# Dilated attention on one core: softmax weights transposed on TensorE and stored as 48 rows of 512 bytes, with buffers of their own for plain v, weight rows and probabilities

## The chip, the cores and the metric

The kernel runs on one core of one Trainium2 chip. The metric is the time of one execution on the device in microseconds (us), as a median over runs.

## The reference, cut to what matters

The program is two blocks of a transformer on 1024 rows of width 1024 in float32. The change lies in the first mixer of the first block, a dilated window attention with 18 heads in three groups of six. Each group has its own window and dilation. The three groups' outputs for one head are weighted by a softmax over the groups' log-sum-exps, multiplied with silu of a gate, and projected:

```
outs, lses = [], []
for g, (window, dil) in enumerate(DIL_GROUPS):          # 3 groups
    o, l = dilated_window_attention(q[:, :, hs], k[:, :, hs], v[:, :, hs], rel_bias[:, hs], window, dil)
    outs.append(o); lses.append(l)
wts = softmax(stack(lses, axis=0), axis=0)              # one weight for each group, row and head
o = concatenate([outs[g] * wts[g][..., None] for g in range(3)], axis=2)
y = o.reshape(B, S, WIDTH_A) * silu(gate)
return y @ w_out
```

The rest of the first block (a second mixer) and the whole second block follow after it and are not touched.

## The kernel before

Each float32 operand of a large product is split into a high and a low part, so that one product is three matmul passes. A weight tile comes by DMA into a raw buffer from one ring of five (`raw()`, shown as `wr`, 128 x 1024), a CAST makes its high part (`wh`, L199, on VectorE = DVE) and a subtraction its low part (`wl`, L203, on GpSimd = POOL or DVE).

The dilated stage walks nine pairs (hp, g): hp = 0, 1, 2 is a pair of heads in each group, g the group. For each pair, `dil_batches` gives a list of jobs (scores, softmax, transposes, values). Between the jobs the program issues "pieces" of other matmul work (`fill`): the q, k, v projection of the next pair, and, once a head pair is through all three groups, its three gates (`dil_gate`: 48 matmuls for each, in two halves of 24, each into one PSUM buffer `g`, of which there are two, then `th` by ScalarE = ACT and `sg` by DVE, L293) and three products (`dil_product`).

For each head pair hp, `dil_weights` reads the statistics of the three groups back from DRAM (`std`, L810), makes the softmax weights in a raw buffer with 16 small DVE operations and an Exp (L813 to L822), and stores them to DRAM (`wtd`, L825) so that each (group, head) is one row of 1024 numbers. In the raw buffer a partition is a row of the sequence within a tile, so that this store writes six times 1024 single numbers. `dil_product` then reads a row back into 64 partitions at a time (L528, two reads for each product), multiplies `sg` with it (L529) and with the attention's output (L530), and stores the result to DRAM (`yTa`, L532). Head pair 0 has its weights made in the first job of hp = 1, head pair 1 in that of hp = 2, and head pair 2 after the last job.

After that the output projection begins. `tail_begin` loads the nine rows of `a_w_out` in 512 KB pieces through the raw ring (L1097), multiplies each by a modulation row (L1098) and splits it. `tail_finish` has for each of eight tiles of 128 rows a `product(t, 0)` over the six early row blocks (head pairs 0 and 1: 36 matmuls of 512 columns) and a `product(t, 1)` over the three late ones (head pair 2: 18 matmuls). Each reads its part of `yTa` back (`yr`, L1157), and ACT casts it (`yh`, L1158).

Two queues set the order: nearly all DMAs are issued by SyncE (SP) in program order, and DVE, ACT, POOL and TensorE (PE) each work through their instructions in order. In order to load ahead, the weights of the following gate or projection are asked for when the one before starts (`next_w`). The lines that matter:

```
def raw(self, shape=None):
    return self.wr.tile(shape or [P, 1024], F32, tag="wr", bufs=5, name=self.nm("wr"))
...
for g in range(3):
    for a in range(2):
        nc.sync.dma_start(wtd[hp, g, a, :].rearrange("(t p) -> p t", p=P), z[:, :, a, g])
```

Of the kernel before, what the change touches and what calls it, by code (L numbers as in the profile page):

```python
# [12 lines left out]
F32 = mybir.dt.float32  # L13
F32R = mybir.dt.float32r
# [127 lines left out]
class Kern:  # L142
# [189 lines left out]
    def phase_A(self, x_in):  # L332
        nc, i = self.nc, self.i
        with ExitStack() as ctx:
# [93 lines left out]
            c1 = ExitStack()  # L428
            self.psum(c1, "", "so")
            ag = self.tags(ctx, "ag")  # L430
            lp = Pools(self.tags(c1, "al", side="right"), {t: ag for t in ("sg", "wb", "xs", "o")})
            yT = self.dr.tile([WA, S], F32, name="yTa")
            std = self.dr.tile([3, S, 12], F32, name="std")
            wtd = self.dr.tile([3, 3, 2, S], F32, name="wtd")
            parts = [([3 * g + hp for g in range(3)], yT.rearrange("(g h p) n -> h g p n", g=3, p=P)[hp])
                     for hp in range(3)]
            w_in = i["a_w_in"][0]
# [37 lines left out]
            for j, (hp, g) in enumerate(groups):  # L475
                jobs = self.dil_batches(lp, hp, g, tbd, std, qkv[j], os)
                pieces = 12
                if hp and g == 0:
                    for gg in range(3):
                        more += [gates[hp - 1, gg], self.dil_product(lp, hp - 1, gg, sgs, os, wtd, yT)]  # L480
                        pieces += 5
                more += [fills[j + 1]] if j < 8 else [gates[2, 0]]
                if j == 8:
                    pieces = 4
                done = 0
                for m, job in enumerate(jobs):
                    n = pieces * (m + 1) // len(jobs) - done
                    step(job, n)
                    if m == 0 and hp and g == 0:
                        self.dil_weights(lp, hp - 1, std, wtd)  # L490
                    done += n
                    next(mods, None)
                if j < 8:
                    fill(100)
            step(None, 0)
            self.dil_weights(lp, 2, std, wtd)
            self.next_w(3 * WA + 2 * 384 + 2 * P)
            self.pin = False
            c1.close()
            ct = ExitStack()  # L500
            tail = self.tail_begin(ct, parts[:2], i["a_w_out"][0], 0, nc.vector)
            for g in range(3):
                for _ in itertools.chain(gates[2, g], self.dil_product(lp, 2, g, sgs, os, wtd, yT)):
                    pass
        return self.tail_finish(ct, tail, parts[2:], i["a_w_out"][0], x_in, 0)

    def dil_gate(self, lp, ut, w_in, hp, g, sgs):
# [14 lines left out]
    def dil_product(self, lp, hp, g, sgs, os, wtd, yT):  # L522

        nc = self.nc
        sg = sgs[hp, g]
        wb = self.raw()
        for a in range(2):
            nc.sync.dma_start(wb[a * 64:(a + 1) * 64, :], wtd[hp, g, a, :].partition_broadcast(64))  # L528
        nc.vector.tensor_tensor(sg, sg, wb, OP.mult)  # L529
        (nc.vector if hp == 2 else nc.gpsimd).tensor_tensor(sg, sg, os[hp, g], OP.mult)  # L530
        c0 = g * 384 + hp * P
        nc.sync.dma_start(yT[c0:c0 + P, :], sg)  # L532
        yield
# [66 lines left out]
    def dil_project(self, lp, ut, w_in, hp, g, res):  # L600


        nc = self.nc
        dil = DILS[g]
        c0 = g * 384 + hp * P

        def perm(ap):
            return ap.rearrange("p (i d) -> p d i", d=dil)

        def flat(ap):  # L610
            return ap.rearrange("p (d i) -> p d i", d=dil)

        hl = S // dil // 2
        halves = [slice(0, hl), slice(hl, 2 * hl)]
        out = res[hp * 3 + g] = []

        def project(c, h, evac, tag):
            w = self.next_w(c)
            self.next_w(c, 1)
            ps = self.pp(tag, 2)  # L620
            for k0 in (0, 4):
                self.gemm_T_half(w, ut, h, ps, kts=range(k0, k0 + 4))
                if k0:
                    evac(h, perm(ps))
                yield

        def tiles(*names):
            return [lp.tile([P, S], F32R, tag=n, bufs=2, name=self.nm(n)) for n in names]

        def split_q(q):  # L630

            def evac(h, ps):
                for r, o, t in zip(rows, rows[::-1], q):
                    nc.scalar.copy(flat(t[r])[:, :, halves[h]], ps[r])
                for r, o, t in zip(rows, rows[::-1], q):
                    nc.vector.tensor_tensor(flat(t[o])[:, :, halves[h]], ps[r],
                                            flat(t[r])[:, :, halves[h]].bitcast(F32), OP.subtract)
            return evac

        def split_k(k, low):  # L640

            def evac(h, ps):
                for r, t in zip(rows, k):
                    nc.scalar.copy(flat(t[r])[:, :, halves[h]], ps[r])
                for r, o, t, u in zip(rows, rows[::-1], k, low):
                    for d in (r, o):
                        nc.vector.tensor_tensor(flat(u[d])[:, :, halves[h]], ps[r],
                                                flat(t[r])[:, :, halves[h]].bitcast(F32), OP.subtract)
                for r, o, t in zip(rows, rows[::-1], k):
                    nc.scalar.copy(flat(t[o])[:, :, halves[h]], ps[r])  # L650
            return evac

        rows = [slice(a * 64, a * 64 + 64) for a in range(2)]
        q, k, low = tiles("q0", "q1"), tiles("k0", "k1"), tiles("kl0", "kl1")
        out += [q, (k, low)]
        evacs = [split_q(q), split_k(k, low)]
        vt = self.raw()
        evacs.append(lambda h, ps: nc.scalar.copy(flat(vt)[:, :, halves[h]], ps))

        first = hp + g == 0  # L660
        order = [(j, h) for h in range(2) for j in range(3)]
        for j, h in order if first else sorted(order):
            yield from project(j * WA + c0, h, evacs[j], "t" if first and (j, h) == (2, 0) else "g")
        vh = lp.tile([P, NT, P], F32R, tag="vh", bufs=2, name=self.nm("vh"))
        vl = lp.tile([P, NT, P], F32R, tag="vl", bufs=2, name=self.nm("vl"))
        out.append((vh, vl))
        for h in range(2):
            tp = self.pp("t", 2, [P, 4, P])
            self.transposes(tp, vt[:, h * 512:(h + 1) * 512], 4)
            self.split(vh[:, h * 4:h * 4 + 4], vl[:, h * 4:h * 4 + 4], tp)  # L670
        yield

    def dil_batches(self, lp, hp, g, tbd, std, qkv, os):
# [72 lines left out]
        class Job:  # L746
# [27 lines left out]
            def transpose(self):  # L774
                rows, nb, nblk = self.rows, len(self.tl), self.nblk
                tp = kern.pp("t", 2, [P, 4, P])
                for j in range(nb):
                    for b in range(nblk):
                        kern.tr(tp[:, j * nblk + b, :rows], self.xs[:rows, j, b * P:(b + 1) * P],
                                kern.ident[:rows, :rows])  # L780
                self.ph = lp.tile([P, 4, P], F32R, tag="pth", bufs=1, name=kern.nm("pth"))
                self.pl = lp.tile([P, 4, P], F32R, tag="ptl", bufs=1, name=kern.nm("ptl"))
                m = nb * nblk
                kern.split(self.ph[:, :m, :rows], self.pl[:, :m, :rows], tp[:, :m, :rows])

# [19 lines left out]
    def dil_weights(self, lp, hp, std, wtd):  # L805

        nc = self.nc
        wb = self.raw()
        st = wb[:, 0:96].rearrange("p (t a g s) -> p t a g s", t=NT, a=2, g=3)
        nc.sync.dma_start(st, std[hp].rearrange("(t p) (a g s) -> p t a g s", p=P, a=2, g=3))  # L810
        mn, zz = (wb[:, c:c + 16].rearrange("p (t a) -> p t a", a=2) for c in (96, 112))
        e, z = (wb[:, c:c + 48].rearrange("p (t a g) -> p t a g", a=2, g=3) for c in (128, 176))
        nc.vector.tensor_reduce(mn, st[:, :, :, :, 0], AX.X, OP.min)  # L813
        for g in range(3):
            nc.vector.tensor_tensor(e[:, :, :, g], mn, st[:, :, :, g, 0], OP.subtract)
        nc.scalar.activation(e, e, AF.Exp)
        for g in range(3):
            nc.vector.tensor_tensor(z[:, :, :, g], e[:, :, :, g], st[:, :, :, g, 1], OP.mult)
        nc.vector.tensor_reduce(zz, z, AX.X, OP.add)
        nc.vector.reciprocal(zz, zz)  # L820
        for g in range(3):
            nc.vector.tensor_tensor(z[:, :, :, g], e[:, :, :, g], zz, OP.mult)  # L822
        for g in range(3):
            for a in range(2):
                nc.sync.dma_start(wtd[hp, g, a, :].rearrange("(t p) -> p t", p=P), z[:, :, a, g])  # L825


    def rope_pairs(self, eng, a, b, cos, sin, pool, shp):
# [1067 lines left out]

# [9 lines left out]
```

## Time and profile before

| what | value |
|---|---|
| median of 3 runs | 4132.61 us (4131.44 to 4135.64) |
| profiled execution, its own time | 4131.9 us |
| its span | 4130.1 us |
| granted TensorE clock, mean | 0.97 of full |
| PE busy | 3858.2 us, 93% of the span |
| DVE busy | 2447.7 us, 59% |
| ACT busy | 1382.1 us, 33% |
| POOL busy | 1085.5 us, 26% |

The profiled execution's own time is 1.8 us above its span and 0.7 us below the median. PE is the engine with the largest share. The dilated stage's part that is touched lies between about 225 and 745 us of the span; what comes after it is 82% of the span.

### The profile page before, as it was taken

To read this page: it belongs to the slowest core of one execution; us is meant where nothing else is said; L and a number is where in the kernel's file an instruction comes from. 1 tells how busy PE (TensorE), PEld (TensorE's weight loads), DVE (VectorE), ACT (ScalarE), POOL (GpSimd) and SP (SyncE) were. 2 spreads that over 40 slices of the span, in tenths; PEclk is the share of its full clock that TensorE was granted. 3 is DMA by queue.
4 is the path that set the end of the run, shared out by engine and by line. 5 is a ranking of instruction groups with operands and counts; after the bars stand their busy time and mean duration, and the time that the engine had idled before them with its cause. 6 is when DMAs were issued, how large, how long until landed. Compare 5 with 4: busy or idle time off the path is not lost. (4 is left out here: it accounts for less than half of the span.)

```text
span 4130.1 us, 54373 instructions
## 1 busy us (share of the span) xinstructions
PE 3858.2 (93%) x21085; PEld 3272.8 (79%) x21085; DVE 2447.7 (59%) x4596; ACT 1382.1 (33%) x2938; POOL 1085.5 (26%) x1016
## 2 busy tenths in 40 slices
PE   7979796899999989999999999997999999999998
PEld 5767675688889867999778888885999778888886
DVE  6645455956777767568754434338568764443436
ACT  3424242124777633256421111113136431111111
POOL 1111111420222322134233232334134232323233
PEclk9989898999999989999999999998999999999999
DMA  6363516220111243111421111113111231111112
GB/s 237 96 82 83 76 41 149 95 86 29 35 25 32 62 120 117 41 38 37 137 83 48 45 51 41 51 50 120 55 42 37 95 115 46 47 46 51 41 51 82
DMA packets 318897, 290.80 MB, mean 70 GB/s; under 512 B 70779, under 2 KB 273267, under 8 KB 318638
## 3 DMA queue, kind: packets, MB, share of 16 engines
q1 hardware_dynamic: 313362, 268.23, 23.5%
q10 hardware_dynamic: 5276, 19.08, 1.5%
q8 instruction: 167, 2.74, 0.3%
q14 instruction: 92, 0.75, 0.1%
HBM read 240.26 MB, written 51.72 MB: 71 GB/s over the span
## 5 line engine op out<-in xcount | busy, mean ns | idle before, releaser
L203 POOL TENSOR_TENSOR wl<-wr,wh 128x1024 fp32r<-128x1024 f32 (+1 forms) x253 | 495.4, 1966 | 1589.6 <-DVE wh L199 1502.8
L199 DVE CAST wh<-wr 128x1024 fp32r<-128x1024 f32 x222 | 181.9, 820 | 751.7 <-PE y L151 310.7
L151 PE MATMUL y<-uh_m,wl 128*128 128x512 f32 x1056 | 417.1, 395 | 4.7 <-DVE z L1631 4.2
L151 PE MATMUL y<-uh_m,wh 128*128 128x512 f32 x1056 | 419.8, 398 | 0.0
L151 PE MATMUL y<-ul_m,wh 128*128 128x512 f32 x1056 | 418.8, 397 | 0.0
L1784 ACT ACTIVATE cv<-y,cw 128x1024 f32<-128x1024 f32 x66 | 79.8, 1209 | 775.7 <-PE y L151 775.7
L151 PE MATMUL g<-uh_a,wl 128*128 128x512 f32 x568 | 236.8, 417 | 55.2 <-DVE sg L293 55.1
L151 PEld LDWEIGHTS y<-uh_m,wl 128*128 128x128 f32 x1056 | 199.0, 188 | 55.1 <-issue 4.6
L151 PEld LDWEIGHTS y<-uh_m,wh 128*128 128x128 f32 x1056 | 199.1, 189 | 48.4
L151 PEld LDWEIGHTS y<-ul_m,wh 128*128 128x128 f32 x1056 | 198.9, 188 | 47.6 <-DVE ul_m L191 0.9
L151 PE MATMUL y<-wo,yh 128*128 128x512 f32 x784 | 219.8, 403 | 17.0 <-ACT yh L1158 17.0
L151 PE MATMUL g<-ul_a,wh 128*128 128x512 f32 x568 | 229.3, 404 | 0.5 <-POOL ul_a L422 0.4
L151 PE MATMUL g<-uh_a,wh 128*128 128x512 f32 x568 | 228.7, 403 | 0.0
L151 PEld LDWEIGHTS y<-wo,yh 128*128 128x128 f32 x784 | 149.2, 193 | 50.7 <-ACT yh L1158 18.5
L191 DVE TENSOR_TENSOR pt<-t,pt 128x512 fp32r<-128x512 f32 x256 | 165.8, 680 | 22.2 <-ACT pt L190 20.4
L151 PE MATMUL y<-wl,hh 128*128 128x512 f32 x440 | 175.4, 399 | 0.0
L151 PE MATMUL y<-wh,hl 128*128 128x512 f32 x440 | 175.1, 398 | 0.0
L151 PE MATMUL y<-wh,hh 128*128 128x512 f32 x440 | 175.1, 398 | 0.0
L151 PEld LDWEIGHTS g<-uh_a,wl 128*128 128x128 f32 x568 | 111.5, 196 | 78.9 <-DVE sg L293 49.5
L995 DVE TENSOR_REDUCE nm<-s 128x1 f32<-128x1024 f32 x128 | 155.7, 1216 | 27.1 <-PE s L151 26.5
L151 PE MATMUL g<-wl,uh_f 128*128 128x256 f32 x576 | 166.4, 289 | 3.0 <-DVE dv L191 2.5
L151 PE MATMUL g<-wl,uh_n 128*128 128x256 f32 x576 | 166.0, 288 | 3.1 <-DVE dv L191 2.5
(446 smaller groups left out, 10312.2 us busy)
## 6 DMA issues: line engine op xcount, KB each, us to landing
wr<-w_up SPq DMA_DIRECT2D x88, 512.0 KB
wr<-ada_w SPq DMA_DIRECT2D x48, 512.0 KB
wr<-w_down SPq DMA_DIRECT2D x44, 512.0 KB
wr<-a_w_in SPq DMA_DIRECT2D x36, 512.0 KB
wr<-w_in SPq DMA_DIRECT2D x24, 512.0 KB
xs<-wr SPq DMA_DIRECT2D x16, 512.0 KB
wr<-xs ACTq DMA_DIRECT2D x16, 512.0 KB
wr<-w_in SPq DMA_DIRECT2D x32, 256.0 KB
```

The source lines that it names most:

```text
L151: ins = self.nc.tensor.matmul(*args, **kw)
L191: nc.vector.tensor_tensor(lo, src, hi.bitcast(F32), OP.subtract)
L199: (self.nc.scalar.copy if act else self.nc.vector.tensor_copy)(hi, raw)
L203: (eng or self.nc.gpsimd).tensor_tensor(lo[..., cs], raw[..., cs], hi[..., cs].bitcast(F32), OP.subtract)
L995: nc.vector.tensor_reduce(nm, sp, AX.X, OP.max, negate=True)
L1784: nc.scalar.activation(t, ps, AF.Identity, bias=cw[:, 3, c:c + 1], scale=cw[:, 2, c:c + 1])
```

## The change

- `dil_weights` works in an own tile `dw` (128 x 224) in place of a raw buffer, and writes the weights so that the 48 numbers of a partition are ordered (group, head, tile).
- The six stores are replaced by a generator `turn`: PE transposes the 128 x 48 weights into PSUM buffer `t`, DVE copies the 48 x 128 result into a tile `dz`, and one DMA stores 48 rows of 512 bytes. `turn` is one more piece of work that is issued behind the first gate of the head pair.
- The weight rows are read into an own single buffer `wb` and no longer into a raw buffer; a projection's plain v lies in an own single buffer `vt`.
- The probabilities' high and low parts (`pth`, `ptl`) have two buffers each in place of one.
- At the end of the stage the order of code was gate 0, product 0, gate 1, product 1, gate 2, product 2 of head pair 2. It is now gate 0, gate 1, `turn`, product 0, product 1, gate 2, product 2.
- A scratch size for dynamic DMAs is given.

Not changed: the 8-byte writes of the statistics to `std`, the read of `std`, the number of matmuls of the products.

```diff
-            lp = Pools(self.tags(c1, "al", side="right"), {t: ag for t in ("sg", "wb", "xs", "o")})
+            lp = Pools(self.tags(c1, "al", side="right"), {t: ag for t in ("sg", "wb", "xs", "o", "dw", "dz")})
...
-            wtd = self.dr.tile([3, 3, 2, S], F32, name="wtd")
+            wtd = self.dr.tile([3, 3, 2, NT, P], F32, name="wtd")
...
                 if hp and g == 0:
+                    turn_w = []
                     for gg in range(3):
                         more += [gates[hp - 1, gg], self.dil_product(lp, hp - 1, gg, sgs, os, wtd, yT)]
                         pieces += 5
+                    more.insert(1, itertools.chain.from_iterable(turn_w))
+                    pieces += 1
...
-                        self.dil_weights(lp, hp - 1, std, wtd)
+                        turn_w.append(self.dil_weights(lp, hp - 1, std, wtd))
...
-            self.dil_weights(lp, 2, std, wtd)
+            turn_w = self.dil_weights(lp, 2, std, wtd)
...
-            for g in range(3):
-                for _ in itertools.chain(gates[2, g], self.dil_product(lp, 2, g, sgs, os, wtd, yT)):
-                    pass
+            last = [self.dil_product(lp, 2, g, sgs, os, wtd, yT) for g in range(3)]
+            for _ in itertools.chain(gates[2, 0], gates[2, 1], turn_w, *last[:2], gates[2, 2], last[2]):
+                pass
...
-        wb = self.raw()
+        wb = lp.tile([P, S], F32, tag="wb", bufs=1, name=self.nm("wb"))
         for a in range(2):
-            nc.sync.dma_start(wb[a * 64:(a + 1) * 64, :], wtd[hp, g, a, :].partition_broadcast(64))
+            nc.sync.dma_start(wb[a * 64:(a + 1) * 64, :], wtd[hp, g, a].rearrange("t p -> (t p)").partition_broadcast(64))
...
-        vt = self.raw()
+        vt = lp.tile([P, S], F32, tag="vt", bufs=1, name=self.nm("vt"))
...
-                self.ph = lp.tile([P, 4, P], F32R, tag="pth", bufs=1, name=kern.nm("pth"))
-                self.pl = lp.tile([P, 4, P], F32R, tag="ptl", bufs=1, name=kern.nm("ptl"))
+                self.ph = lp.tile([P, 4, P], F32R, tag="pth", bufs=2, name=kern.nm("pth"))
+                self.pl = lp.tile([P, 4, P], F32R, tag="ptl", bufs=2, name=kern.nm("ptl"))
...
-        wb = self.raw()
+        wb = lp.tile([P, 224], F32, tag="dw", bufs=1, name=self.nm("dw"))
...
-        e, z = (wb[:, c:c + 48].rearrange("p (t a g) -> p t a g", a=2, g=3) for c in (128, 176))
+        e = wb[:, 128:176].rearrange("p (t a g) -> p t a g", a=2, g=3)
+        z = wb[:, 176:224].rearrange("p (g a t) -> p t a g", a=2, g=3)
...
-        for g in range(3):
-            for a in range(2):
-                nc.sync.dma_start(wtd[hp, g, a, :].rearrange("(t p) -> p t", p=P), z[:, :, a, g])
+
+        def turn():
+
+            ps = self.pp("t", 2)
+            self.tr(ps[:48, :P], wb[:, 176:224], self.ident)
+            rows = lp.tile([48, P], F32, tag="dz", bufs=1, name=self.nm("dz"))
+            nc.vector.tensor_copy(rows, ps[:48, :P])
+            nc.sync.dma_start(wtd[hp].rearrange("g a t p -> (g a t) p"), rows)
+            yield
+
+        return turn()
...
-    nc = bacc.Bacc("TRN2", target_bir_lowering=False, num_devices=1)
+    nc = bacc.Bacc("TRN2", target_bir_lowering=False, num_devices=1, dynamic_dma_scratch_size=1024)
```

The first place is SP's queue around the weights of head pair 0. The numbers in a name only tell one buffer from another; `wr_2313` before and `wr_2324` after are the same load, the weights of the gate (0, 2). Before, from the statistics' last writes on:

```order
L744 DMA std<-stats_1745 512x1x2
L217 DMA wr_2162<-a_w_in 128x8x128
L744 DMA std<-stats_1745 512x1x2
L810 DMA wr_2216<-std 128x8x12
L825 DMA wtd<-wr_2216 128x8x1 x6
L528 DMA wr_2281<-wtd 64x1024 x2
L217 DMA wr_2313<-a_w_in 128x8x128
L528 DMA wr_2407<-wtd 64x1024 x2
```

The same stretch of SP's queue in the changed kernel, whose read of the statistics is L813, store L834 and read of the weight rows L531:

```order
L217 DMA wr_2324<-a_w_in 128x8x128
L560 DMA wr_2436<-ada_b 1x1024
L696 DMA T_2142<-tbd 128x384
L747 DMA std<-stats_1748 512x1x2 x2
L545 DMA wr_2515<-ada_w 128x1024
L813 DMA dw_2222<-std 128x8x12
L545 DMA wr_2567<-ada_w 128x1024
L737 DMA std<-stats_2141 64x2
L738 DMA std<-stats_2141 64x2
L834 DMA wtd<-dz_2286 48x128
L217 DMA wr_2594<-a_w_in 128x8x128
L531 DMA wb_2318<-wtd 64x1024 x2
```

The gate's weight load stood behind the six stores and the first read of weight rows; it now stands ahead of the last writes of the statistics.

The second place is SP's queue at the end of the stage. Before, it runs from the first row of `a_w_out` on:

```order
L1097 DMA wr_5345<-a_w_out 128x1024
L825 DMA wtd<-wr_5299 128x8x1 x6
L1097 DMA wr_5355<-a_w_out 128x1024
L1097 DMA wr_5362<-a_w_out 128x1024
L1097 DMA wr_5369<-a_w_out 128x1024
L1097 DMA wr_5376<-a_w_out 128x1024
L1157 DMA yr_5568<-yTa 128x3x128
L1097 DMA wr_5383<-a_w_out 128x1024
L1157 DMA yr_5568<-yTa 128x3x128
L528 DMA wr_5390<-wtd 64x1024 x2
```

In the changed kernel the first four rows of `a_w_out` (L1109 there) have been issued further up; from the last writes of the statistics on, SP has:

```order
L747 DMA std<-stats_5065 512x1x2 x2
L1109 DMA wr_5388<-a_w_out 128x1024
L813 DMA dw_5309<-std 128x8x12
L1109 DMA wr_5549<-a_w_out 128x1024
L1109 DMA wr_5559<-a_w_out 128x1024
L1109 DMA wr_5566<-a_w_out 128x1024
L1169 DMA yr_5633<-yTa 128x3x128 x2
L834 DMA wtd<-dz_5454 48x128
L531 DMA wb_5457<-wtd 64x1024 x2
L1169 DMA yr_5828<-yTa 128x3x128 x2
L531 DMA wb_5463<-wtd 64x1024
L535 DMA yTa<-sg_5099 128x1024
```

All nine loads of `a_w_out` now stand ahead of the store of the weights, where eight stood behind the six stores.

The third place is DVE's queue at the end of the stage, in the changed kernel, from the seventh row of `a_w_out` (L1110 is the product with the modulation row) to the copy of the turned weights (L833); ahead of it, behind the last split of probabilities (`ptl`, L191), stand a subtraction L203, L817, two more L1110 and the three L819:

```order
L1110 TENSOR_TENSOR wr_5549<-wr_5549,wr_5348 128x1024
L822 TENSOR_TENSOR dw_5309<-dw_5309 128x8x2 x3
L199 CAST wo_5391<-wr_5388 128x1024
L823 TENSOR_REDUCE dw_5309<-dw_5309 128x16
L203 TENSOR_TENSOR wo_5392<-wr_5388,wo_5391 128x1024
L824 RECIPROCAL dw_5309<-dw_5309 128x16
L293 SCALAR_TENSOR_TENSOR sg_5397<-th_5422,g_5395 128x512
L826 TENSOR_TENSOR dw_5309<-dw_5309 128x8x2 x3
L1110 TENSOR_TENSOR wr_5559<-wr_5559,wr_5348 128x1024
L1110 TENSOR_TENSOR wr_5566<-wr_5566,wr_5348 128x1024
L1172 TENSOR_TENSOR yl_5589<-yr_5581,yh_5585 128x384 x2
L833 COPY dz_5454<-t_5452 48x128
```

Before, the small operations on the weights followed the last `ptl` at once, with no work on `a_w_out` between them; now the copy stands behind five L1110, one CAST and two L203.

## Rows read from the trace of the kernel before

**Rows 1.** Page: busy time of each engine over the whole span.

```profile
PE 3858.2 (93%) x21085; PEld 3272.8 (79%) x21085; DVE 2447.7 (59%) x4596; ACT 1382.1 (33%) x2938; POOL 1085.5 (26%) x1016
```

**Rows 2.** Timeline, PE (start us, us, instruction [idle before <-releaser]), waits over 4 us.

```profile
237.67 1.11 PE L156 MATMUL t<-ident,xs 128*128 128x128 f32 x4 [6.61 <-DVE vl L191]
...
275.28 0.79 PE L151 MATMUL g<-uh_a,wl 128*128 128x512 f32 x1 [14.82 <-DVE sg L293]
...
491.12 0.79 PE L151 MATMUL g<-uh_a,wl 128*128 128x512 f32 x1 [18.70 <-DVE sg L293]
...
655.45 0.77 PE L151 MATMUL g<-uh_a,wl 128*128 128x512 f32 x1 [6.82 <-DVE sg L293]
...
677.91 0.79 PE L151 MATMUL g<-uh_a,wl 128*128 128x512 f32 x1 [14.71 <-DVE sg L293]
...
705.79 2.07 PE L151 MATMUL y<-wo,yh 128*128 128x512 f32 x4 [11.23 <-ACT yh L1158]
...
725.70 2.08 PE L151 MATMUL y<-wo,yh 128*128 128x512 f32 x4 [4.54 <-ACT yh L1158]
```

**Rows 3.** Windows: us, busy time of each engine, granted clock, DMA share, GB/s.

```profile
core 0: us, PE busy (x) PEld busy (x) DVE busy (x) ACT busy (x) POOL busy (x), PEclk, DMA share, GB/s
247.92:253.66 5.74, 5.74 (x30) 4.73 (x28) 1.42 (x3) 2.62 (x6) 0.00 (x0) 1.00 1.95 1
655.45:660.45 5.00, 5.00 (x13) 3.97 (x14) 0.00 (x0) 0.00 (x0) 1.07 (x1) 0.57 1.06 1
...
677.91:682.91 5.00, 5.00 (x12) 3.94 (x13) 5.00 (x5) 1.01 (x2) 1.74 (x1) 0.50 0.46 127
```

**Rows 4.** Timeline, DVE, head pair 0's gates, and the same wait of head pair 1.

```profile
273.93 0.69 DVE L199 CAST wh<-wr 128x1024 fp32r<-128x1024 f32 x1 [23.55 <-DMA wr<-a_w_in]
274.54 0.68 DVE L293 SCALAR_TENSOR_TENSOR sg<-th,g 128x512 f32<-128x512 f32 x1
...
291.97 0.69 DVE L199 CAST wh<-wr 128x1024 fp32r<-128x1024 f32 x1 [1.25 <-DMA wr<-a_w_in]
...
489.78 0.69 DVE L199 CAST wh<-wr 128x1024 fp32r<-128x1024 f32 x1 [27.47 <-DMA wr<-a_w_in]
```

**Rows 5.** Timeline, SP's queue, head pair 0 (start us, us spent issuing).

```profile
232.29 0.38 SPq L810 DMA_DIRECT2D wr<-std  x1
236.88 11.72 SPq L825 DMA_DIRECT2D wtd<-wr  x6
...
253.93 0.67 SPq L217 DMA_DIRECT2D wr<-a_w_in  x1
...
288.04 0.39 SPq L217 DMA_DIRECT2D wr<-a_w_in  x1
```

**Rows 6.** DMA view of the stretch from 238 to 262 us.

```profile
DMA packets 5920, 0.16 MB, mean 7 GB/s; under 512 B 5886, under 2 KB 5886, under 8 KB 5920
```

**Rows 7.** Timeline, SP's queue, the end of the stage.

```profile
643.20 12.53 SPq L825 DMA_DIRECT2D wtd<-wr  x6
655.83 13.65 SPq L1097 DMA_DIRECT2D wr<-a_w_out  x4
...
697.32 0.33 SPq L532 DMA_DIRECT2D yTa<-sg  x1
```

**Rows 8.** Timeline, DVE and ACT, the end of the stage.

```profile
637.25 0.69 DVE L191 TENSOR_TENSOR ptl<-t,pth 128x512 fp32r<-128x512 f32 x1 [0.48 <-ACT pth L190]
...
671.77 1.23 DVE L1098 TENSOR_TENSOR wr<-wr,wr 128x1024 f32<-128x1024 f32 x1 [16.47 <-DMA wr<-a_w_out]
...
709.11 0.51 ACT L1158 CAST yh<-yr 128x384 fp32r<-128x384 f32 x1 [2.73 <-DMA yr<-yTa]
```

**Rows 9.** Timeline: DVE's first operation on the read statistics; far later, another 64-partition row load and its first reader.

```profile
234.55 0.20 DVE L813 TENSOR_REDUCE wr<-wr 128x16 f32<-128x48 f32 x1 [1.78 <-DMA wr<-std]
...
1363.55 0.45 SPq L1042 DMA_DIRECT2D wr<-rdb  x1
1367.61 2.40 POOL L1043 TENSOR_TENSOR sg<-sg,wr 128x1024 f32<-128x1024 f32 x1 [36.47 <-DMA wr<-rdb]
```

## The prediction

> **What bounds the kernel now.** I read the page first: PE is busy 93% of the span [rows 1], so time is won where PE waits, hardly elsewhere. Then I read PE's timeline for waits over 4 us in the dilated stage and its tail, since the change touches nothing else. There are nine; seven stand in [rows 2]. The eighth is the twin of the first in head pair 1, and the ninth comes after the tail, beyond the change. I asked who ends each. Four times it is DVE's `sg` (L293), the last step of a gate, without which the PSUM buffer `g` is not free; twice it is ACT's `yh`, the cast of attention rows read back; the other is DVE's `vl`.
>
> DVE's timeline says why `sg` is late [rows 4]. At 273.93 a CAST of weights ends an idle time of 23.55 us that a weight load ended, and `sg` stands right behind it. DVE works in order, so `sg` was held by a weight tile that it doesn't use. Head pair 1 shows the same CAST after 27.47 us.
>
> SP's queue says why the load is late [rows 5]. The six stores of the weights take 11.72 us to issue from 236.88, and the load for that CAST goes out at 253.93 and is used at 273.93: 20.0 us. The same load issued at 288.04 is used at 291.97: 3.9 us. Between lies what the DMA view shows: 5920 packets in 24 us, nearly all under 512 bytes, at 7 GB/s [rows 6]. The DMA engines are full of 4-byte writes, and the raw buffer that they read stays taken.
>
> At the end of the stage the stores take 12.53 us to issue and the next four loads of `a_w_out` another 13.65 us [rows 7]; the second of those rows reaches DVE after 16.47 us of idling [rows 8].
>
> Each wait has a second price. In the first 5 us after it the granted clock is 0.50 or 0.57 [rows 3], the lower level of 1.2 GHz for all or most of it. PE was at 1.00 while it was busy before the wait. Those 5 us do 2.5 to 2.85 us of work, so each wait costs about 2.4 us more (2.2 to 2.5).
>
> **The change part by part.** What can be had from [rows 2] is:
> - head pair 0: 14.82 + 2.4 = 17.2 us;
> - head pair 1: 18.70 + 2.4 = 21.1 us;
> - tail: 6.82 + 14.71 + 11.23 + 4.54 = 37.3, with four dips of 2.4, 46.9 us.
>
> The wait at 237.67, and its twin in head pair 1, is on `vl` behind the small operations that wait for the read of `std`. The change leaves this read and the 8-byte statistics alone, so I keep both waits.
>
> *Head pairs 0 and 1.* One store of 48 rows of 512 bytes takes the place of 6144 writes of 4 bytes. Issue falls from 11.72 us to about the 0.4 of one plain DMA [rows 5]. The order moves the gate's load ahead of the last statistics, and `dw` and `wb` are no raw buffers, so nothing of the weights holds the ring. I therefore take both waits away in full. Added: one transpose, a quarter of the four that took 1.11 us at the lower clock [rows 2], and a copy of 48 x 128, under the 0.69 us of the CAST of 128 x 1024 [rows 4]. Both sit between other matmul work. What remains is new: one `wb` buffer serves three products, and a product's multiplication stands in DVE's queue ahead of CASTs and `sg`. A load of such rows takes 4.1 us from issue to use when quiet [rows 9]. A gate half is 5.74 us of PE work [rows 3], and two halves, 11.5 us, lie between products, so most is covered. I take 1.5 us for each head pair, between 0 (all covered) and 4.1 (one load uncovered). Terms: 15.7 and 19.6 us.
>
> *Tail, what goes.* The nine loads of `a_w_out` now go ahead of the store, so the waits of 6.82 and 14.71 should go. The last two, on `yh`, depend on how soon head pair 2's products land.
>
> *Tail, what comes.* The preparation of `a_w_out` moves between the last jobs: three L1110 of 1.23 us [rows 8], a CAST of 0.69 and an L203 of about 1.2, 5.6 us of DVE work, in a stretch where DVE still had waits. I take 2 us of it on the path (bounds 0 and 5.6).
>
> The store is late. Behind the last `ptl`, which ends at 637.9 [rows 8], DVE has five L1110, one CAST, two L203, `sg` and some 3 us of small operations: 13 us, and about 2 us of waits, so the copy ends near 653. Then:
> - issue 0.9 and landing 2.3, as for the read of `std` issued at 232.29 and used at 234.55 [rows 5, 9]: 656.2;
> - two loads into `wb`, 0.45 + 4.1 [rows 9]: 660.7;
> - two multiplications of 1.23: 663.2;
> - two more rounds, since `wb` is single: each 0.45 + 4.1 + 2 x 1.23 = 7.0: 677.2;
> - store to `yTa` and read back: 11.8 from 697.32 to 709.11 before [rows 7, 8]. DMA was busy there; I take 9 (6.3, twice the 2.3 and a cast, at best): 686.2.
>
> Meanwhile PE came to its first wait at 655.45 - 6.82 = 648.6 [rows 2]. With 2 us of delay, 0.3 for the transpose, the two remaining gate halves (11.5) and the early products of two tiles (2 x 36 matmuls, 16.4 us at 0.228 each, within the 0.19 to 0.24 that 5.74 us for 24 matmuls of a half, 30 with others, give in [rows 3]) it is at 679. The late rows come at 686.2: a wait of 7.2 us, plus one dip of 2.4. Multiplications and casts crowd DVE there; I put 1.5 us on that (0 to 4). Tail: 46.9 - 2 - 7.2 - 2.4 - 1.5 = 33.8 us. Ends: 44 if the chain is hidden, 18 if its rounds cost 11 us each.
>
> *Edits costed at nothing.* Two buffers for `pth` and `ptl`: no wait in [rows 2] is ended by them, since the gates' matmuls lie between transposes and values; if that cover were gone, one split of 0.69 us [rows 8] a job would show. `vt`: it takes one user out of the ring; its single buffer is read within its own projection, under the twelve pieces of matmul work. The scratch size: the page lists no DMA issued by POOL.
>
> *Sum.* 15.7 + 19.6 + 33.8 = 69.1 us. From the profiled 4131.9 that leaves 4062.8; the median lies 0.7 higher, so 4063.5, rounded to 4064. After 745 us the program is as before; I put nothing on it.
>
> **A rule beside it.** The Trainium skill, "DMA: Bandwidth & Descriptors", section "Rules for kernel authors", says that a strided last dimension lowers to one descriptor per element and should be made contiguous. The trace agrees: 5886 of 5920 packets are under 512 bytes [rows 6]. By the same rule the 8-byte statistics are left as they were, which is the rival "no change" below.
>
> **Rivals.**
> 1. *The chain is hidden (12%).* If the copy comes a few us sooner, or store and read back take 6.3 us, the late rows are there when PE is at 679. Then the 7.2 and the 2.4 go too: 4064 - 9.6 = 4054. For it: DVE's queue behind 637.9 is mostly idle waits today. Against it: nine loads of 512 KB precede the store in SP's queue. The same page's section "Anatomy of one DMA — SWDGE (gpsimd) path" puts a fixed 2.0 us on a DMA issued from GpSimd, mostly the wait until the last byte has landed. As an estimate, with that for each of the five DMAs here, the chain would end about where this rival puts it; the SP loads of [rows 9] took longer.
> 2. *The chain is no faster than today's traffic (17%).* With the DMA engines full of `a_w_out`, each of the three rounds takes 11 instead of 7 us and the read back the full 11.8: 12 + 2.8 later, so 4064 + 15 = 4079, up to 4092 with waits on `wb` in the head pairs. For it: the 13.65 us of four loads' issue [rows 7]. Against it: that jam was made by 4-byte writes.
> 3. *DVE stalls on `wb` (8%).* Six products of head pairs 0 and 1 wait 3 to 4 us each in DVE's queue, and `sg` behind them: 6 x 3.5 = 21, so about 4085, 4100 at most. Against it: 11.5 us of cover for a load of 4.1.
> 4. *It doesn't do what it says (3%).* The statistics' 6144 writes of 8 bytes per head pair are as many as the removed ones. If they, not the weights' stores, keep the DMA engines full, the gate's load is as late as ever: 4132. Against it: the load at 253.93 went out behind the weights' stores, 17 us after the statistics had been read.
> 5. *Slower (4%).* The single `wb` makes nine loads serial, each with DVE's queue behind it. The gain of 68 us is used up when 9 x (L - 11.5) = 68, that is from a load time L of 19.1 us. The weight load under the scatter did take 20.0 us [rows 4, 5]: with L = 20 to 21 the time is 4140 to 4150. Against it: that was with 4-byte writes in the queues.
>
> **How the numbers follow.** The forecast, 4050 to 4080, has 56%; the rivals have 12, 17, 8, 3 and 4%. From 4044 to 4096 the range takes in the forecast, most of rivals 1 and 2, and part of 3, and leaves out about 13 in 100. A change of 0.2%, 8.3 us, is about what a measurement of this kernel can tell from none. Faster by more: 56 + 12 + 17 + 8 = 93%; within: 3%; slower: 4%.
>
> **What would show it.** In PE's timeline the waits near 275, 491, 655 and 678 are gone or under 3 us, and those on the read of `std` near 237 and 450 remain at 6 to 8 us (the rest comes earlier by what was won before it). In SP's queue the store is one row of about 0.4 us. No CAST of weights waits over 5 us on `a_w_in` there. In the tail one wait of about 7 us on `yh` stands before the first late product, with a clock of 0.50 behind it. I am wrong if the gate's load is still used 10 us or more after its issue (rival 4), if DVE's L532 has waits of several us on the weight rows (rivals 3, 5), or if the time after the tail differs by more than 3 us.

## The result and the profile after

The changed kernel takes 4079.95 us (median of 4, 4074.51 to 4081.00), against 4133.53 us before (median of 4). The ratio is 0.9867, 95% interval 0.9852 to 0.9881: about 54 us or 1.3% faster. The forecast was 4064, 16 us too low, inside the range. The profiled execution is the fastest of the four, 4074.51 us with a span of 4072.7, so its trace shows 57.4 us of gain.

TensorE's timeline of the changed kernel has these waits where [rows 2] had its own (start us, us, instruction, [idle before <- releaser]):

```profile
234.07 1.12 PE L156 MATMUL t<-ident,vt 128*128 128x128 f32 x4 [4.46 <-ACT vt L661]
237.25 1.12 PE L156 MATMUL t<-ident,xs 128*128 128x128 f32 x4 [1.63 <-DVE vl L191]
272.37 1.09 PE L156 MATMUL t<-ident,xs 128*128 128x128 f32 x4 [3.48 <-DVE wr L568]
...
576.00 1.11 PE L156 MATMUL t<-ident,xs 128*128 128x128 f32 x4 [3.25 <-DVE vl L191]
601.51 0.27 PE L151 MATMUL o<-pth,vl 128*64 128x128 f32 x1 [2.86 <-ACT pth L190]
605.06 0.37 PE L151 MATMUL o<-ptl,vh 128*64 128x128 f32 x1 [1.92 <-DVE ptl L191]
658.65 2.05 PE L151 MATMUL y<-wo,yh 128*128 128x512 f32 x4 [14.15 <-ACT yh L1170]
```

The four waits on `sg` are gone. The two on the read of the statistics stay, here as 4.46 + 1.63. A wait of 3.48 us is new among head pair 0's gates. Three small waits that were not there come before the end of the stage. One wait of 14.15 us on late rows stands in the tail.

SP's queue and DVE's timeline for head pair 0 answer to [rows 4, 5]. The store takes 0.33 us to issue, and no CAST waits for a load: the one at 251.90 was idle 3.33 us for TensorE.

```profile
229.65 0.38 SPq L813 DMA_DIRECT2D dw<-std  x1
...
253.50 0.33 SPq L834 DMA_DIRECT2D wtd<-dz  x1
```

```profile
232.65 0.20 DVE L817 TENSOR_REDUCE dw<-dw 128x16 f32<-128x48 f32 x1 [6.42 <-DMA dw<-std]
...
251.90 0.69 DVE L199 CAST wh<-wr 128x1024 fp32r<-128x1024 f32 x1 [3.33 <-PE g L151]
```

Where the time came from is read from windows that begin at 0: after the length of the window stand TensorE's busy time and, as (x), the number of its instructions. At equal counts (the changed kernel has one transpose more for each head pair) the two kernels are at the same place. Before, and then after:

```profile
0.00:222.00 222.00, 191.59 (x1071) 153.54 (x1071) 145.20 (x212) 95.60 (x212) 35.56 (x23) 0.98 0.49 157
0.00:432.00 432.00, 373.29 (x2094) 303.60 (x2095) 252.49 (x376) 171.04 (x394) 72.32 (x38) 0.95 0.49 121
0.00:545.00 545.00, 456.49 (x2528) 371.18 (x2529) 300.59 (x452) 202.28 (x470) 93.21 (x46) 0.93 0.50 111
0.00:600.00 600.00, 507.56 (x2824) 414.21 (x2825) 327.71 (x495) 225.46 (x521) 100.32 (x49) 0.93 0.47 105
0.00:632.00 632.00, 539.43 (x3049) 441.98 (x3050) 343.14 (x520) 243.13 (x569) 102.73 (x50) 0.94 0.45 101
0.00:645.00 645.00, 552.35 (x3126) 452.68 (x3127) 349.06 (x538) 249.83 (x582) 103.15 (x51) 0.94 0.45 101
0.00:764.00 764.00, 633.75 (x3443) 517.09 (x3444) 429.26 (x638) 264.97 (x609) 133.54 (x62) 0.92 0.47 108
```

```profile
0.00:221.24 221.24, 192.45 (x1071) 153.99 (x1072) 145.84 (x212) 95.48 (x212) 35.57 (x23) 0.98 0.49 160
0.00:414.72 414.72, 372.56 (x2095) 303.37 (x2095) 250.93 (x376) 171.00 (x394) 72.90 (x38) 0.97 0.41 127
0.00:505.51 505.51, 454.03 (x2530) 369.84 (x2531) 300.25 (x454) 202.10 (x470) 92.99 (x46) 0.96 0.40 123
0.00:555.20 555.20, 501.87 (x2826) 410.25 (x2826) 326.14 (x497) 225.11 (x521) 100.15 (x49) 0.97 0.39 118
0.00:592.91 592.91, 536.33 (x3051) 440.04 (x3051) 346.85 (x525) 242.69 (x569) 105.81 (x51) 0.96 0.37 113
0.00:613.25 613.25, 551.90 (x3128) 452.35 (x3129) 364.11 (x544) 253.33 (x588) 114.23 (x54) 0.96 0.38 113
0.00:701.69 701.69, 625.54 (x3446) 511.61 (x3447) 428.92 (x640) 264.17 (x609) 135.34 (x62) 0.95 0.39 118
```

The differences of the window ends give the time gained up to each place, and their steps the gain of each stretch:

| stretch (time before, us) | gained up to its end | in it | forecast |
|---|---|---|---|
| to 222 | 0.8 | 0.8 | 0 |
| to 432, head pair 0's gates | 17.3 | 16.5 | 15.7 |
| to 545, head pair 1's gates | 39.5 | 22.2 | 19.6 |
| to 600, jobs of head pair 2 | 44.8 | 5.3 | 0 |
| to 632, the last jobs | 39.1 | -5.7 | -2, with the next row |
| to 645, the very last | 31.8 | -7.3 | |
| to 764, tail | 62.3 | 30.5 | 35.8 |
| the rest of the span | 57.4 | -4.9 | 0 |

The forecast's 33.8 us for the tail are split here into its 2 us of delay in the last jobs and 35.8.

### The profile page after: what moved, and what is told of

Same layout as the page of the kernel before. It is cut to its first block, busy times and chain, and to the rows that moved or that the text cites. A ratio compares the mean times of both kernels' runs of the same rounds, so it can differ in the third digit from the quotient of the medians.

```text
span 4072.7 us, 54330 instructions
## 1 busy us (share of the span) xinstructions
PE 3848.7 (95%) x21088; PEld 3265.4 (80%) x21088; DVE 2455.7 (60%) x4599; ACT 1381.1 (34%) x2938; POOL 1089.9 (27%) x1016
## 3 DMA queue, kind: packets, MB, share of 16 engines
q8 instruction: 167, 2.74, 0.3%
## 5 line engine op out<-in xcount | busy, mean ns | idle before, releaser
L203 POOL TENSOR_TENSOR wl<-wr,wh 128x1024 fp32r<-128x1024 f32 (+1 forms) x253 | 498.2, 1977 | 1461.5 <-DVE wh L199 1393.6
L191 DVE TENSOR_TENSOR pt<-t,pt 128x512 fp32r<-128x512 f32 x256 | 165.9, 681 | 22.5 <-ACT pt L190 20.8
L151 PE MATMUL v<-pt,v 128*64 128x256 f32 (+1 forms) x1024 | 154.9, 294 | 11.1 <-DVE o L1042 11.0
```

The lines of the kernel that those rows point to most:

```text
L151: ins = self.nc.tensor.matmul(*args, **kw)
L191: nc.vector.tensor_tensor(lo, src, hi.bitcast(F32), OP.subtract)
L203: (eng or self.nc.gpsimd).tensor_tensor(lo[..., cs], raw[..., cs], hi[..., cs].bitcast(F32), OP.subtract)
```

## The experiments

Every run had its kernel before beside it; since that median differs between the sets of runs (4121 to 4134 us), ratios are compared. All ratios carry a 95% interval of about +-0.0015. The changed kernel stands at 0.9867.

**1. Only the store put back.** The theory is that the 4-byte packets make the loads late; the rival is that the weights held buffers of the ring.

```diff
-            self.tr(ps[:48, :P], wb[:, 176:224], self.ident)
...
-            nc.sync.dma_start(wtd[hp].rearrange("g a t p -> (g a t) p"), rows)
+            for g in range(3):
+                for a in range(2):
+                    nc.sync.dma_start(wtd[hp, g, a].rearrange("t p -> p t"), z[:, :, a, g])
```

> The changed kernel with only the store put back: six stores of 1024 single numbers in place of transpose, copy and one store of 48 rows; own buffers and the new order stay. Theory (the 4-byte packets keep the DMA engines and SP's queue busy, so that weight loads land late): most of the gain goes, 4110 to 4135 us, with waits of over 8 us on sg in the gates of head pairs 0 and 1. Rival (the raw buffers held by the weights were the cause, and own buffers cure that): 4075 to 4092 us, no such waits.

Measured: 0.9995 (0.9986 to 1.0004): all of the gain is gone. In its timelines (SP, DVE, PE) the stores again take 10.71 us to issue. Now the first load of weight rows is late, 14.75 us, and TensorE waits on `ptl`, which stands behind that product in DVE's queue:

```profile
236.98 10.71 SPq L832 DMA_DIRECT2D wtd<-dw  x6
...
269.72 1.22 DVE L532 TENSOR_TENSOR sg<-sg,wb 128x1024 f32<-128x1024 f32 x1 [14.75 <-DMA wb<-wtd]
...
272.20 0.37 PE L151 MATMUL o<-ptl,vh 128*64 128x128 f32 x1 [12.32 <-DVE ptl L191]
487.92 0.37 PE L151 MATMUL o<-ptl,vh 128*64 128x128 f32 x1 [17.03 <-DVE ptl L191]
```

In the tail two waits on `yh` of 16.14 and 15.44 us stand. So the scattered store is the cause; whether the full DMA engines or the long issue in SP's queue cost more was not tried apart. The expected wait on `sg` did not return in that form, since the gate's load now stands ahead of the stores in SP's queue.

**2. Weights back in the ring.** The same question from the other side.

```diff
-        wb = lp.tile([P, S], F32, tag="wb", bufs=1, name=self.nm("wb"))
+        wb = self.raw()
...
-        wb = lp.tile([P, 224], F32, tag="dw", bufs=1, name=self.nm("dw"))
+        wb = self.raw()
```

> The changed kernel with the weights' work tile and the weight rows back in the ring of five raw buffers; transposed store, own buffer for v and new order stay. Theory (packets are the cause): within 8 us of the changed kernel, 4072 to 4088 us, since a raw buffer is now held for some 5 us only. Rival (held raw buffers are the cause): 4095 to 4125 us, with the CAST of the gate's weights waiting over 8 us on its load.

Measured: 0.9839 (0.9825 to 0.9852), faster than the changed kernel by 0.28% or 12 us, with intervals that meet at 0.9852, and beyond what either theory gave. The ring was not the cause, and the own buffers cost time.

**3. Two buffers for weight rows; 4. one buffer for probabilities.** The second is the first's partner, since room had to be made.

```diff
-                self.ph = lp.tile([P, 4, P], F32R, tag="pth", bufs=2, name=kern.nm("pth"))
+                self.ph = lp.tile([P, 4, P], F32R, tag="pth", bufs=1, name=kern.nm("pth"))
...
-        wb = lp.tile([P, S], F32, tag="wb", bufs=1, name=self.nm("wb"))
+        wb = lp.tile([P, S], F32, tag="wb", bufs=2, name=self.nm("wb"))
```

> The changed kernel with two buffers for the weight rows, and one for each part of the probabilities to make room; to be set against the run with one buffer for each part of the probabilities alone. Theory (the single buffer strings the three late products one behind the other): the wait of 14 us on yh in the tail falls to 7 us or less, 6 to 9 us faster than that run. Rival (the late store of the weights and DVE's queue set it): the wait stays at 12 us or more and the time within 3 us of that run.

> The changed kernel with one buffer for each part of the probabilities, as in the kernel before. Theory (the prediction's zero for this edit): within 3 us of the changed kernel, 4074 to 4083 us. Rival (the second buffers give the 2 to 5 us by which the changed kernel is ahead between head pairs 0 and 2 beyond the removed waits): 4082 to 4088 us.

Measured: 0.9850 with two row buffers, 0.9865 without; the wait on `yh` is 6.99 against 14.07 us, and the medians differ by 5.6 us. So the single buffer does string the late products, as the wait shows; the gain in time lies just under the 6 to 9 us expected, and the intervals overlap. One buffer for probabilities gives 0.9865 against 0.9867: the prediction's zero holds.

**5. The store alone.** From the kernel before: transpose, copy, one store, the layout and the scratch size; `turn` is that of the change, on a raw buffer.

```diff
-                nc.sync.dma_start(wtd[hp, g, a, :].rearrange("(t p) -> p t", p=P), z[:, :, a, g])
+            nc.sync.dma_start(wtd[hp].rearrange("g a t p -> (g a t) p"), rows)
...
-                for _ in itertools.chain(gates[2, g], self.dil_product(lp, 2, g, sgs, os, wtd, yT)):
+                for _ in itertools.chain(gates[2, g], turn_w if g == 0 else (),
+                                         self.dil_product(lp, 2, g, sgs, os, wtd, yT)):
```

> The kernel before with one part of the change alone: transpose, copy and one store of 48 rows of 512 bytes. The ring of five raw buffers, one buffer for each part of the probabilities, plain v in the ring and the old order at the end stay. Theory (the 4-byte packets alone made the waits, and the other parts bring nothing or cost): 55 to 70 us faster than before, a ratio of 0.983 to 0.987. Rival (own buffers or the new order are needed as well): 20 to 45 us faster, 0.989 to 0.995, with a wait of over 8 us on sg or yh left.

Measured: 0.9887 (0.9872 to 0.9902), about 49 us: between the two expectations, and with waits of 10.27 and 5.51 us on `yh` left. The store alone brings some 85% of the change's gain (0.0113 of 0.0133). In its trace the place that is at 545 us before comes 39.3 us earlier (39.5 in the changed kernel), so the gain of both head pairs is the store's.

**6. Weight rows alone in the ring.** The work tile keeps its own buffer.

```diff
-        wb = lp.tile([P, S], F32, tag="wb", bufs=1, name=self.nm("wb"))
+        wb = self.raw()
```

> The changed kernel with only the weight rows back in the ring; the weights' work tile keeps its own buffer. Theory (the single buffer for weight rows is the costly part, through the late products and through the rows of a_w_out that come too early for DVE): 5 to 12 us faster than the changed kernel, a ratio to before of 0.983 to 0.986, and a wait on yh in the tail of under 8 us. Rival (the work tile is the part that costs): within 2 us of the changed kernel, 0.9865, and the wait of 14 us stays.

Measured: 0.9851 (0.9836 to 0.9866), some 6.5 us faster than the changed kernel, though the intervals touch. DVE's three products with weight rows then follow each other, with one wait for the first row alone:

```profile
621.79 1.23 DVE L532 TENSOR_TENSOR sg<-sg,wr 128x1024 f32<-128x1024 f32 x1 [7.67 <-DMA wr<-wtd]
...
624.20 1.22 DVE L532 TENSOR_TENSOR sg<-sg,wr 128x1024 f32<-128x1024 f32 x1
...
628.72 1.23 DVE L532 TENSOR_TENSOR sg<-sg,wr 128x1024 f32<-128x1024 f32 x1
```

**7. The old order at the end.**

```diff
-            for _ in itertools.chain(gates[2, 0], gates[2, 1], turn_w, *last[:2], gates[2, 2], last[2]):
+            for _ in itertools.chain(gates[2, 0], turn_w, last[0], gates[2, 1], last[1], gates[2, 2], last[2]):
```

> The changed kernel with the order at the end as it was: gate and product in turn, the transpose behind the first gate. Theory (order of code at the end counts little, since DVE's queue and the single buffer set when the products come): within 4 us of the changed kernel, ratio 0.9855 to 0.9877. Rival (the new order hides the chain): 6 us slower or more, over 0.988, with a longer wait on yh.

Measured: 0.9874 (0.9857 to 0.9892): no difference that can be told. The wait on `yh` is 5.79, and one of 3.62 us for the transpose is new; the two are 4.7 us less than 14.15, but no gain shows in the ratio.

**8. Later weights.** The prediction kept two waits on the read of the statistics. Here the weights' operations of head pairs 0 and 1 come one job later, behind that job's scores:

```diff
+                if late:
+                    turn_w.append(self.dil_weights(lp, late - 1, std, wtd, job))
...
+        if job:
+            nc.vector.tensor_copy(wb[:job.rows, 96:97], job.head.nmx[:job.rows, job.col:job.col + 1])
         nc.vector.tensor_reduce(mn, st[:, :, :, :, 0], AX.X, OP.min)
```

> The changed kernel with the weights' small operations of head pairs 0 and 1 one job later: a one-column copy of the next job's maxima into the work tile, which is overwritten, makes the first of them wait for that job's scores, by when the statistics have been read. Theory (the two waits that the change left, near 234 and 429 us, are DVE and ACT held by the read of the statistics, with a clock dip behind each): both vanish, 12 to 18 us faster than the changed kernel, ratio to before 0.9822 to 0.9838. Rival (they only move, to the gates or to the next job's scores): within 4 us of the changed kernel.

Measured: 0.9838 (0.9823 to 0.9852), some 12 us faster than the changed kernel. The first operation no longer waits (DVE), and the transpose that waited 1.63 us behind 4.46 waits 0.73 (PE):

```profile
241.98 0.15 DVE L818 COPY dw<-stats 128x1 f32<-128x1 f32 x1
242.16 0.20 DVE L819 TENSOR_REDUCE dw<-dw 128x16 f32<-128x48 f32 x1
...
231.89 0.66 PE L156 MATMUL t<-ident,xs 128*128 128x128 f32 x4 [0.73 <-DVE vl L191]
```

**9. Plain v back in the ring.**

```diff
-        vt = lp.tile([P, S], F32, tag="vt", bufs=1, name=self.nm("vt"))
+        vt = self.raw()
```

> The changed kernel with plain v back in the ring of raw buffers. Theory (the prediction's zero for this edit): within 3 us of the changed kernel, ratio to before 0.986 to 0.9875. Rival (plain v held in the ring delays weight loads all through the stage, which is why the store alone gives some 8 us less than the changed kernel): 0.988 to 0.990.

Measured: 0.9882 (0.9868 to 0.9895). As a time this touches the changed kernel's interval. The windows say more: from 2530 to 2826 instructions (545 to 600 us before) it takes 54.98 us, as before (55.0), where the changed kernel took 49.69:

```profile
0.00:506.16 506.16, 450.45 (x2530) 367.93 (x2531) 297.90 (x454) 201.69 (x470) 92.86 (x46) 0.97 0.40 120
0.00:561.14 561.14, 501.44 (x2826) 410.86 (x2827) 325.06 (x497) 224.81 (x521) 99.99 (x49) 0.96 0.37 112
```

So the 5.3 us of that stretch belong to the own buffer for v. A wait on `vl` goes with it: 2.58 us at 563.92 before, 2.64 at 525.26 in number 9, none there in the changed kernel.

**10. Later weights and rows in the ring; 11. the same with GpSimd; 12. both weights' tiles in the ring.** Number 10 joins numbers 6 and 8. Number 11 moves the modulation products of the first six rows of `a_w_out`, and the low parts of every second one, from VectorE to GpSimd, which had the other low parts already. Number 12 joins numbers 2 and 8.

```diff
-            tail = self.tail_begin(ct, parts[:2], i["a_w_out"][0], 0, nc.vector)
+            tail = self.tail_begin(ct, parts[:2], i["a_w_out"][0], 0, nc.gpsimd)
```

> Later weights (as in the run with the small operations one job later) and weight rows in the ring, together. Theory (the two are in different places, so they add): ratio 0.9815 to 0.9828, that is 16 to 21 us faster than the changed kernel. Rival (the late products take back what was won before them): 0.9835 or more.

> The run before it, with the products of the first six rows of a_w_out with the modulation row and their low parts on GpSimd in place of VectorE. Theory (this work in VectorE's queue holds up the last jobs' splits, for which TensorE waits twice, some 5 us and a clock dip, and it delays the copy of the turned weights): those waits fall below 1.5 us and the time by 5 to 10 us more, ratio 0.979 to 0.981. Rival (GpSimd, at about 2.0 to 2.4 us for each operation, makes the rows late and the early products wait): same or slower than the run before it, 0.982 to 0.985.

> Later weights, with both the weight rows and the weights' work tile in the ring. Theory (a raw buffer taken by the work tile keeps two rows of a_w_out from coming in before the last jobs are done, so VectorE is free for their splits): no wait over 2 us on pth or ptl before the tail, ratio 0.980 to 0.982. Rival (the ring is too short again, and a gate's or the tail's loads come late): 0.983 or more, with a wait of over 4 us on sg.

Measured: 0.9809 (0.9796 to 0.9823), 0.9823 (0.9810 to 0.9836) and 0.9807 (0.9794 to 0.9820). Numbers 10 and 12 are the fastest versions, 79 and 80 us faster than before, and clear of the changed kernel's interval; the two parts add. In number 12 no wait on `pth` or `ptl` stands at the end of the jobs, as expected, but two of some 3.3 us on `sg` do, and 7.19 and 3.33 us on `yh`. Number 11 went the rival's way: its median is 5.3 us above that of number 10, though the intervals overlap. Its timelines of POOL, ACT and PE show why: ACT's CAST of a row now waits for GpSimd, and `pth` stands behind it in ACT's queue.

```profile
578.92 2.33 POOL L1112 TENSOR_TENSOR wr<-wr,wr 128x1024 f32<-128x1024 f32 x1
...
581.28 1.04 ACT L199 CAST wo<-wr 128x1024 fp32r<-128x1024 f32 x1 [7.77 <-POOL wr L1112]
582.24 0.58 ACT L190 CAST pth<-t 128x512 fp32r<-128x512 f32 x1
...
582.87 0.37 PE L151 MATMUL o<-pth,vl 128*64 128x128 f32 x1 [8.38 <-ACT pth L190]
```

## Why the prediction was right, and where it was off

**Right: the chain from packets to TensorE.** The stores fill the DMA engines and SP's queue, loads land late, DVE waits in order, TensorE waits for DVE. Number 1 shows it by undoing the store, number 5 by doing the store alone. The terms of head pairs 0 and 1, 15.7 and 19.6 us, measured 16.5 and 22.2. For head pair 0 this is partly luck: `wb` cost more than the 1.5 us allowed. L532 waits 1.99 and 2.73 us for its rows there, TensorE waits 3.48 us at 272.37 behind the second, and its granted clock is 0.50 in the next 5 us. What made up for it was not counted either: the wait of 2.42 us on `vl` at 344.69 before is gone.

The kept waits on the read of the statistics are there, and number 8, which moves the operations that wait for this read, takes both away. Rival 4 (no effect) and rival 5 (slower) did not come. Rival 3 came in part: L532 waits 2.0 to 3.0 us four times in the two head pairs and 4.40 and 4.57 us in the tail, which the prediction named as a sign of being wrong, but no wait of several us on `sg` follows in those gates. The time of 4080 is that of rival 2, but not its mechanism: the rounds took 8.7 and 9.2 us and not 11, store and read back 8.25 and not 11.8, and the loads of `a_w_out` were all issued before the chain began.

**Off: "I take 2 us of it on the path".** The work on `a_w_out` in the last jobs cost more than the upper bound of 5.6 us. It was larger, to begin with: four L1110, not three, two CASTs and an L203 stand ahead of the last `ptl`, and they took 12.8 us. DVE's and ACT's timelines of the changed kernel show it: two L1110 take 4.51 us, `vl` stands behind them, and TensorE waits 3.25 us at 576; an ACT CAST that waits for L1110 holds `pth`, and TensorE waits 2.86 us at 601.51, then 1.92 for a `ptl` behind a DVE CAST of 2.74 us.

```profile
570.84 4.51 DVE L1110 TENSOR_TENSOR wr<-wr,wr 128x1024 f32<-128x1024 f32 x2
575.27 1.27 DVE L191 TENSOR_TENSOR vl<-t,vh 128x512 fp32r<-128x512 f32 x2
...
599.93 1.05 ACT L199 CAST wo<-wr 128x1024 fp32r<-128x1024 f32 x1 [2.22 <-DVE wr L1110]
600.88 0.58 ACT L190 CAST pth<-t 128x512 fp32r<-128x512 f32 x1
...
601.66 2.74 DVE L199 CAST wo<-wr 128x1024 fp32r<-128x1024 f32 x1
604.33 0.68 DVE L191 TENSOR_TENSOR ptl<-t,pth 128x512 fp32r<-128x512 f32 x1
```

Together that is 8.0 us of waits, and the clock falls behind them: 0.50 in the 5 us from 576. The time gained falls from 44.8 us to 39.1 over the first wait and to 31.8 over the other two: 13 us in place of 2. The prediction had counted DVE's busy time as the price; it is paid by what stands behind in two in-order queues. With fewer free buffers in the ring (number 2) the wait at 576 and those on `pth` and `ptl` don't appear, though two on `sg` of 2.66 and 3.49 us do. Number 6, which differs from number 2 only by the own buffer of the work tile `dw`, has all three again (3.25, 2.84 and 2.46 us). So it is this buffer, taken out of the ring, that lets the work on `a_w_out` come early.

**Off: "a wait of 7.2 us".** It is 14.15. The steps of the late chain, in DVE's and SP's timelines:

```profile
619.91 0.27 DVE L833 COPY dz<-t 48x128 f32<-48x128 f32 x1
...
629.93 1.23 DVE L532 TENSOR_TENSOR sg<-sg,wb 128x1024 f32<-128x1024 f32 x1 [4.40 <-DMA wb<-wtd]
...
638.67 2.44 DVE L532 TENSOR_TENSOR sg<-sg,wb 128x1024 f32<-128x1024 f32 x1
...
647.89 1.22 DVE L532 TENSOR_TENSOR sg<-sg,wb 128x1024 f32<-128x1024 f32 x1 [4.57 <-DMA wb<-wtd]
```

```profile
621.07 0.43 SPq L834 DMA_DIRECT2D wtd<-dz  x1
...
650.40 0.33 SPq L535 DMA_DIRECT2D yTa<-sg  x1
```

The copy ends at 620.2, which is 659.3 on the old scale (with the 39.1 gained by 632), 6.3 later than the 653 forecast. From the copy's end to the first product 9.7 us pass (forecast 7.7); the next two products begin 8.7 and 9.2 us after the one before (7.0 each). In the first of these rounds casts, an L203 and `sg` lie between the products in DVE's queue; in the second the product itself takes 2.44 us, and its successor's rows come 5.1 us after their last load was issued at 642.78. From the last store's issue to TensorE's start at 658.65 it is 8.25 (9). The chain is 38.5 us long against 33.2. TensorE came to the place at 644.5, which is 683.6 on the old scale, 4.6 later than the forecast 679; the waits of 2.86 and 1.92 us lie in between. So 6.3 + 5.3 - 4.6 = 7.0 us are added to the forecast wait of 7.2. Number 3 halves the wait with a second buffer, and number 6 leaves 2.74 and 3.43 us of it. The tail as a whole gave 5.3 us less than its forecast, and these 7.0 more than account for it. (The estimate in rival 1 counts five DMAs in this chain; there are six: two stores, the rows of three products and one read back.)

**Off: `vt` costed at nothing.** Its own buffer is worth 5.3 us between 545 and 600 (number 9). I looked for waits over 4 us only, and plain v's share was in smaller ones on `vl`: the one of 2.58 us, with a granted clock of 0.66 in the 5 us behind it, is most of the 5.3 (some 4.3, as an estimate: 2.58 and a third of 5).

**Off: "I put nothing on it" after the tail.** 4.9 us are lost there: at 764 the gain is 62.3, at the end 57.4. This is over the 3 us that the prediction named as a sign of being wrong. The largest steps are in two places, one in each round of the program's last loop over layers; they cost some 3.5 and 4.2 us, and smaller steps elsewhere give part of it back. TensorE has two waits on `u` there after and one on `z` before (timeline, PE, first place, after and then before):

```profile
2036.98 1.09 PE L156 MATMUL t<-ident,u 128*128 128x128 f32 x8 [2.48 <-ACT u L1656]
...
2048.08 1.09 PE L156 MATMUL t<-ident,u 128*128 128x128 f32 x8 [1.80 <-ACT u L1656]
```

```profile
2100.29 0.76 PE L151 MATMUL y<-uh_m,wl 128*128 128x512 f32 x1 [2.11 <-DVE z L1631]
```

The same steps appear in the traces of numbers 1, 5 and 10, so neither the transposed store nor the own buffers are needed for them. Numbers 1 and 5 have in common of the change only the store's later place in the program, the layout of the weights and the scratch size. The prediction put the scratch size at nothing, and no run tries it alone. That the steps come from another order of ACT's work there is argued, not tried: the cause stays open. The last 3.8 us between the trace (57.4) and the medians (53.6) have no place, as only the fastest execution has a trace.

## What to carry to other kernels

The store whose inner run was one element was paid here by whoever shared the DMA engines and the issuing queue, and in the end by TensorE, which has nothing to do with it: look for the late load, then for what stands behind its reader. When a stall is removed, ask what work moves up into the freed buffers, and price it by the splits and casts that stand behind it in in-order queues, not by its busy time. A freed buffer is no gain by itself: the own buffer for v brought 5.3 us, that of the work tile let other work come too early, and the single one for weight rows strung three products that the shared ring lets overlap.

## What the runs showed of the hardware that was not expected

- A product on DVE lasted longer beside work on GpSimd. The two L1110 that took 4.51 us began at 570.84, while GpSimd ran one L203 of 3.26 us from 571.01; two L1110 in one row from 616.70, with no GpSimd work beside them, took 2.35 us. The prediction had 1.23 us for each. The Trainium skill, "SBUF — State Buffer", section "SBUF: two separate sides", says that VectorE with two SBUF inputs and a GpSimd operation that reads SBUF exclude each other at a shared port pair. These rows agree.

```profile
571.01 3.26 POOL L203 TENSOR_TENSOR wl<-wr,wh 128x1024 fp32r<-128x1024 f32 x1 [11.93 <-DVE wh L199]
...
616.70 2.35 DVE L1110 TENSOR_TENSOR wr<-wr,wr 128x1024 f32<-128x1024 f32 x2
```

- Short waits cost clock too. Behind the wait of 3.25 us at 576 the granted clock was 0.50 for 5 us, as behind the long ones of [rows 3]. From 566 to 571, while TensorE was busy without a gap, it had been 1.00.

```profile
576.00:581.00 5.00, 5.00 (x14) 4.13 (x15) 2.49 (x4) 2.23 (x9) 0.00 (x0) 0.50 0.46 155
```
